# In-projection of the second block: operand sums, stores and loads regrouped among the engines

## The chip, the cores and the metric

The kernel runs on one core of a Trainium2 chip. The metric is the device time of one execution in microseconds (us), the median over several runs. The profile is that of one execution, read by engine: PE multiplies matrices (PEld loads its stationary operand), DVE is VectorE, ACT is ScalarE, POOL is GpSimd, SP is SyncE, which here only starts DMAs.

## What is computed

Two transformer blocks in sequence over 1,024 tokens of width 1,024, all in float32. Only the start of the second block matters here. With `x` the first block's output after its final norm:

```
hx = modulate(rmsnorm(x, norm1_g), sh1, sc1)
q, k, v, u, b, c, ga, gc = split(hx @ w_in)      # 1024, 256, 256, then 5 x 1024 columns
q, k = axial_rope(q), axial_rope(k)              # rotation
z = c * u;  y = b * conv3(z)                     # short convolution over tokens
a = (y @ w_proj_conv) * sigmoid(gc) + (attention(q, k, v) @ w_proj_attn) * sigmoid(ga)
x = x + g1 * (a @ w_out)                         # the residual is x itself
```

Attention over windows and a mixture of experts follow; they are not touched.

## The kernel before

**Float32 by three products.** Each operand is split into a high part, which ACT writes (line 58), and a remainder, which DVE writes (line 59); `mm3` (lines 65 to 67) adds three matmuls of 128x128 by 512. Weights arrive in the order of a list written by hand: `Weights.fill` has SP load the next 512 KB into one of four raw slots as soon as an earlier one has been split, `conv` splits the next piece, and `get` splits until `1 + ahead` pieces are ready and hands out one. The split pieces turn in a ring of three buffers, so a buffer comes free when PE has used the piece three before. Every engine works through its own instructions in the order of the program, and a DMA that SP or POOL starts waits its turn there.

**Order of the stage.** `x1` holds the first block's output, transposed, eight tiles of 128x1024.
1. `natural` for the 256 context rows: four pieces of K, a callback `mid` after some of them. After the second piece `x1_rs` makes row factors; after the third `hx_first` spreads one of them over a tile (`spread`: eight PE transposes into two PSUM banks, two ACT copies) and begins `hx`, the split modulated input, eight pairs of 128x1024 (lines 1238 to 1251).
2. A second row factor is spread to `rs1b` (line 1285), behind all of `hx` on ACT.
3. `natural` for keys and values (line 1317): 8 PSUM banks, one for each 128 tokens, four pieces of 48 matmuls, then `ev_kv` for each bank: DVE rotates the keys out of PSUM (lines 1292, 1296), POOL adds the two terms (line 1297) and starts the store, ACT copies the values.
4. `x1n` (line 1314): DVE scales the eight `x1` tiles by `rs1b`, and SP stores them as the residual. `x1`'s memory then goes to `TQ`, the operands of step 6.
5. `natural` twice for the queries, 512 columns each, with `ev_q` at the end of each (rotation as in 3, 512 wide; the tiles of the two terms and of the sum have two buffers each). In the first of the two, `quarters(k)` follows each of the four pieces: POOL adds high and low part of `hx` back together (line 1331, two of 128x1024) and forms four differences of quarters (line 1334, 128x512), which ACT and DVE split into `TQ`.
6. `quads` (line 1352): two blocks of 128 columns against all tokens with seven products instead of eight (Strassen's scheme in Winograd's form). Each product is 12 matmuls into a bank of its own; the banks turn through all eight. `SEVEN` says which quarters or sums each uses; the matching sums of the weights are made by `seven` on POOL: `make2` (lines 153, 154) for products 2 and 3, `make3` (158) for product 4, `make4` (162) for product 5. `W.ahead` goes to 4 ahead of the first `quads`.
7. Twenty calls of `quads`, the last four for the attention gate. In the last one `y_split` follows products 0 to 3: it splits a tile of `y` and calls `y_load`, in which POOL starts the load of the next one into the buffer that came free (one `y`, one `z`). The rest of the eight tiles follows after it. POOL's next DMAs load the keys and queries for the attention (`kn`, `qn`, lines 1502, 1503); SP's load the gate of the convolution (`gc_load`, line 1456), which `ev_mc` on DVE multiplies (line 1460). PE goes on with `y @ w_proj_conv`, first two column blocks with K as the outer loop (line 1516), then one block at a time.

Of the kernel before, what the change touches and what calls it, by code (L numbers as in the profile page):

```python
# [8 lines left out]
F32 = mybir.dt.float32  # L9
# [5 lines left out]
OP = mybir.AluOpType  # L15
# [3 lines left out]
P = 128  # L19
# [3 lines left out]
def fused(tc, x, mix_norm_g, w_in, b_f, sgu_ln_g, sgu_ln_b, w_s, b_s, out_norm_g, w_out,  # L23
# [4 lines left out]
    nc = tc.nc  # L28
# [3 lines left out]
    T, D = x.shape[1], x.shape[2]  # L32
    NT = T // P
    KD = D // P
    TH = T // 512
    EPS = 1e-6
    ACT, DVE, POOL, PE = nc.scalar, nc.vector, nc.gpsimd, nc.tensor
    act = nc.scalar.activation
    ES = ExitStack()
    L, R = "left", "right"  # L40

    def pool(es, name, bufs=1, side=L, space=None):
        kw = dict(name=name, bufs=bufs)
        if space is not None:
            kw["space"] = space
        else:
            kw["side"] = side
        return es.enter_context(tc.tile_pool(**kw))
# [4 lines left out]
    def rd(ap):  # L53
        return ap.bitcast(F32)

    def split(h, l, src, scale=None):
        if scale is None:
            act(h, src, AF.Copy)  # L58
            DVE.tensor_tensor(l, src, rd(h), op=OP.subtract)  # L59
        else:  # L60
            act(h, src, AF.Copy, scale=scale)
            DVE.scalar_tensor_tensor(l, src, scale, rd(h), op0=OP.mult, op1=OP.subtract)

    def mm3(ps, lh, ll, rh, rl, start, stop):
        PE.matmul(ps, lh, rh, start=start, stop=False)  # L65
        PE.matmul(ps, lh, rl, start=False, stop=False)  # L66
        PE.matmul(ps, ll, rh, start=False, stop=stop)  # L67
# [134 lines left out]
    def wsrc(w, k0, kc, c0, n):  # L202
        return w[k0 * P:(k0 + kc) * P, c0:c0 + n].rearrange("(k p) n -> p k n", p=P)
# [25 lines left out]
    def cols(n):  # L229
        a = small[:, nsm[0]:nsm[0] + n]  # L230
        nsm[0] += n
        assert nsm[0] <= 320
        return a
# [29 lines left out]
    def spread(dst, col, pts=None):  # L263

        for h in range(2):
            pt = pts[h] if pts else psb.tile([P, 512], F32, name="b")
            for t in range(4):
                PE.transpose(pt[:, t * P:(t + 1) * P], col[:, 4 * h + t:4 * h + t + 1].to_broadcast([P, P]), ident)
            act(dst[:, h * 512:(h + 1) * 512], pt, AF.Copy)
# [72 lines left out]
    W = Weights(es_a, units, stage=0, scols=1056)  # L342
# [12 lines left out]
    for src in (mix_norm_g, out_norm_g, ffn_norm_g, norm1_g_2, norm2_g_2, conv_w_2, b_mod_2, c_2, c_ctx_2):  # L355
        n = 1
# [102 lines left out]
    def natural(W, lH, lL, pieces, n, evac, nt=NT, mid=()):  # L459

        pss = [psb.tile([P, 512], F32, name="b") for _ in range(nt)]
        k0, K = 0, sum(pieces)
        for p, kc in enumerate(pieces):
            wh, wl = W.get()
            for t in range(nt):
                for kk in range(kc):
                    k = k0 + kk
                    mm3(pss[t][:, :n], lH(k, t), lL(k, t), wh[:, kk, :], wl[:, kk, :], k == 0, k == K - 1)
            k0 += kc
            if p in mid:  # L470
                mid[p]()
        for t in range(nt):
            evac(t, pss[t][:, :n])
# [49 lines left out]
    for g4 in range(2):  # L523
# [3 lines left out]
        o = slice(g4 * 4, g4 * 4 + 4)  # L527
# [382 lines left out]
    for i in range(NPART):  # L910
        n = -(-(FF - f0) // (NPART - i))
# [41 lines left out]
    es_x1 = ExitStack()  # L953
# [12 lines left out]
    for k in (6, 7):  # L966
        nc.sync.dma_start(raws[k], d_sgu[k - 4])
    groups = ((0, 3), (3, 3), (6, 2))
    W = Weights(es_m, [(wsrc(w_out, k0, kc, c0 * P, n * P), "k", 2) for c0, n in groups
                       for k0, kc in (((4, 4), (0, 4)) if c0 else ((6, 2), (0, 4)))],  # L970
                stage=2, scols=1536, pcols=768, name="w2")
# [50 lines left out]
    W = W3  # L1022
# [9 lines left out]
    es_f = ExitStack()  # L1032
    phh = pool(es_f, "phh", 5)
    for f in late:
        f(phh.tile([P, T], F32, name="hH")[:, :512])
    es_mo = ExitStack()
    rsb = s1

    def ffn_rs():
# [45 lines left out]
    def fw_done():  # L1085
        nonlocal psg, pmo
        es_fw.close()
        psg = pool(es_f, "psg", 2)
        pmo = pool(es_mo, "pmo", 2)

    psg = pmo = None
    for f0, n in parts:
        hT = []
        for f in range(f0, f0 + n):
# [20 lines left out]
            else:  # L1115
                columns_k(W, 2, xh, xhl, range(KD), lambda c, hf, ps: (ev_gate, ev_up)[c](hf, ps),
                          mid={(FM[0], 1): ffn_rs, (FM[1], 1): lambda: (spread(rsb, rs1), fw_done()), (FM[2], 1): lambda: W.prime(1)})
# [10 lines left out]
        mod_sum(modr.popleft())  # L1128
    assert not modq
    es_mo.close()  # L1130
    es_s1.close()


# [70 lines left out]
    d_y = dram.tile([KD, P, T], F32, name="d_y")  # L1204
# [6 lines left out]
    hx = []  # L1211
    ss3 = cols(16)
    rs3 = cols(16)
# [21 lines left out]
    def hx_mul(k, cs):  # L1235
        if k not in tmps:
            tmps[k] = tf("hH")
        DVE.scalar_tensor_tensor(tmps[k][:, cs], x1[k][:, cs], F1[:, k:k + 1], rsxb[:, cs], op0=OP.mult, op1=OP.mult)

    def hx_split(k, cs):  # L1240
        tmp, b1 = tmps[k][:, cs], B1[:, k:k + 1]
        if len(hx) == k:
            hx.append((xt(F32R), xt(F32R)))
        h, l = [a[:, cs] for a in hx[k]]
        if k in HP:
            act(tmp, tmp, AF.Identity, bias=b1)
            act(h, tmp, AF.Copy)
            POOL.tensor_tensor(l, tmp, rd(h), op=OP.subtract)
        else:
            act(h, tmp, AF.Identity, bias=b1)  # L1250
            DVE.scalar_tensor_tensor(l, tmp, b1, rd(h), op0=OP.add, op1=OP.subtract)

    whole = slice(0, T)
    HP = (3, 6)
    hs = [slice(0, 512), slice(512, 1024)]
    def hx_first():
        spread(rsxb, rs3[:, 8:])
        for c in hs:
            hx_mul(0, c)
        for c in hs:  # L1260
            hx_split(0, c)
        hx_mul(1, whole)

    natural(W, lambda k, t: hcH[:, k, t * P:(t + 1) * P], lambda k, t: hcL[:, k, t * P:(t + 1) * P], (2,) * 4, 512,
# [16 lines left out]
    rs_ = prp.tile([P, NT, 64], F32, name="rs", bufs=1)  # L1281
    nc.gpsimd.dma_start(rc, ropec_h)
    nc.gpsimd.dma_start(rs_, ropes_h)
    rs1b = pool(es_x1, "prs1", 1, R).tile([P, T], F32, name="rs1b")
    spread(rs1b, rs3[:, :8])

    def rope(dst, t, ps, nh):
        n = nh * 64
# [10 lines left out]
    hl_ = lambda k, t: hx[k][0][:, t * P:(t + 1) * P]  # L1299
    hll = lambda k, t: hx[k][1][:, t * P:(t + 1) * P]  # L1300
# [7 lines left out]
    def ev_q(c, t, ps):  # L1308
        qo = prp.tile([P, 512], F32, name="qo")
        rope(qo, t, ps, 8)  # L1310
        nc.gpsimd.dma_start(d_q[:, t, c:c + 512], qo)

    def x1n(k):
        DVE.scalar_tensor_tensor(x1[k], x1[k], fngT[:, k:k + 1], rs1b, op0=OP.mult, op1=OP.mult)  # L1314
        nc.sync.dma_start(d_x1T[k], x1[k])

    natural(W, hl_, hll, (2,) * 4, 512, ev_kv)
    for k in range(KD):
        x1n(k)
    es_x1.close()  # L1320


# [2 lines left out]
    TQ = [[pT.tile([P, 4, 512], F32R, name=f"T{i}{c}") for c in "hl"] for i in range(1, 5)]  # L1325

    def quarters(k):
        tr = prp.tile([P, 4, 512], F32, name="tr", bufs=1)
        for i in range(2):
            h, l = hx[k + 4 * i]  # L1330
            POOL.tensor_tensor(tr[:, 2 * i:2 * i + 2, :].rearrange("p i n -> p (i n)"), rd(h), rd(l), op=OP.add)  # L1331
        a11, a12, a21, a22 = [tr[:, i, :] for i in range(4)]
        for o, x, y in ((a11, a12, a11), (a12, a22, a12), (a22, a22, a11), (a21, a21, a22)):
            POOL.tensor_tensor(o, x, y, op=OP.subtract)
        for (h, l), t in zip(TQ, (a11, a22, a12, a21)):
            split(h[:, k, :], l[:, k, :], t)

    for c in (0, 512):
        natural(W, hl_, hll, (2,) * 4, 512, lambda t, ps: ev_q(c, t, ps),
                mid={} if c else {i: (lambda i=i: quarters(i)) for i in range(4)})  # L1340
    es_rp.close()


# [27 lines left out]
    def plus(o, s, b):  # L1371
        DVE.tensor_tensor(o, s, b, op=OP.add)
        return o
# [3 lines left out]
    for j in range(8):  # L1377
# [9 lines left out]
        y = pcv.tile([P, T], F32, name="y")  # L1387
# [14 lines left out]
    def y_load():  # L1402
        k = len(ys) + len(yraw)
        t = pcv.tile([P, T], F32, name="y") if k % 2 else pcv.tile([P, T + 2], F32, name="z")[:, :T]
        nc.gpsimd.dma_start(t, d_y[k])
        yraw.append(t)

    def y_split():
        ys.append((xt(F32R), xt(F32R)))
        split(*ys[-1], yraw.popleft())  # L1410
        if len(ys) + len(yraw) < KD:
            y_load()

    for j in range(4):
        ga, gb = [pcv.tile([P, T], F32, name="g", bufs=2) for _ in range(2)]
        g1, g2 = half("c1"), half("c2")
        mid = {}
        if j == 3:

            W.ahead = 2  # L1420
            mid = {i: (lambda: y_split()) for i in range(4)}
        quads(lambda s, b: act(ga[:, h0], plus(g1, s, b), AF.Sigmoid), lambda s, b: act(ga[:, h1], plus(s, s, b), AF.Sigmoid),
              lambda s, b: act(gb[:, h0], plus(s, s, b), AF.Sigmoid), lambda s, b: act(gb[:, h1], plus(g2, s, b), AF.Sigmoid), mid)
        for i, g in enumerate((ga, gb)):
            nc.gpsimd.dma_start(d_ga[2 * j + i], g)
        if j == 1:
            y_load()
            y_load()
# [519 lines left out]
    for r in range(P // 8):  # L1948
        o = slice(8 * r, 8 * r + 8)
# [123 lines left out]
    for t in range(NT + 2):  # L2073
        if t < NT:
            for c in hs:
                ps = psb.tile([P, 512], F32, name="b")
# [75 lines left out]
```

## Time and profile before

| | before |
|---|---|
| median of 3 runs (lowest to highest) | 3036.11 us (3034.88 to 3037.55) |
| the profiled execution: its time / span | 3037.48 / 3035.7 us |
| mean granted clock of PE | 0.976 of full speed |
| busy: PE / DVE / ACT / POOL | 2868.3 (94%) / 1900.1 (63%) / 1361.9 (45%) / 649.0 (21%) us |
| HBM read / written | 380.62 / 58.23 MB |

The span runs from the first to the last instruction; the time is 1.78 us longer. Starts below are us from the span's start. The work of steps 1 to 7 above begins at about 1230 us, the last `quads` ends at about 1812 us. In a list of waits each line gives who waited, for whom, the total us, the number of times and the longest one. In a timeline: start, duration, engine, line, what it writes and reads, and in brackets how long the engine had been idle and what released it.

### The profile page before, as it was taken

What the parts mean: (1) busy time and instruction counts of PE and PEld (TensorE: products, weight loads), DVE (VectorE), ACT (ScalarE), POOL (GpSimd) and SP (SyncE); (2) the same over time, 40 slices, a digit from 0 to 9 for tenths busy, and PEclk for the clock granted to TensorE, in tenths of its full rate; (3) what the DMA queues carried; (4) which work ended last, traced back from release to release, by engine and by line L of the source; (5) the groups of instructions that cost most, each with busy time, mean ns of one, the idle gap of its engine ahead of it and who ended that gap; (6) DMA issues with size and microseconds to landing.
All of it is one profiled execution on the core that took longest, in us unless ns stands there. A gap on an engine that the chain in (4) does not pass through costs nothing.

```text
span 3035.7 us, 37203 instructions
## 1 busy us (share of the span) xinstructions
PE 2868.3 (94%) x13943; PEld 2392.6 (79%) x13943; DVE 1900.1 (63%) x2717; ACT 1361.9 (45%) x2127; POOL 649.0 (21%) x639
## 2 busy tenths in 40 slices
PE   9999999999999999868999998899899879999997
PEld 7987878888888888756888877777778668888885
DVE  4446944645344445554666652789742479999998
ACT  5346933111121113320322231688721368888886
POOL 2201312000000001275444421133221301211113
PEclk9999999999999999988999999999999889999999
DMA  5120141222232222232222246000253589999998
GB/s 198 36 77 22 41 148 49 90 84 94 72 100 75 92 83 63 76 118 84 83 84 84 83 156 230 25 15 22 71 181 137 194 313 368 377 371 378 377 377 288
DMA packets 295236, 441.27 MB, mean 145 GB/s; under 512 B 14300, under 2 KB 143040, under 8 KB 294928
## 3 DMA queue, kind: packets, MB, share of 16 engines
q1 hardware_dynamic: 276896, 375.54, 35.8%
q0 software_dynamic: 16672, 62.31, 6.0%
q8 instruction: 109, 1.79, 0.2%
q10 hardware_dynamic: 1488, 1.06, 0.1%
q14 instruction: 71, 0.58, 0.1%
HBM read 380.62 MB, written 58.23 MB: 145 GB/s over the span
## 4 chain that ended last, share of the span: by engine, by line
PE 80%; DVE 8%; ACT 4%; POOL 3%; DMA 3%; issue 3%; SPq 0%; POOLq 0%; ACTq 0%; DVEq 0%
PE b L65 23%; PE b L67 23%; PE b L66 23%; PE pt L1612 2%; PE b L1993 1%; PE po L1642 1%; DVE wl L59 1%; PE po L1643 1%; PE pt L777 1%; POOL qo L1297 1%; DVE x L1314 1%; POOL tr L1331 1%; DVE qs L1497 1%; DVE pl L1630 0%; PE sp L1582 0%
## 5 line engine op out<-in xcount | busy, mean ns | idle before, releaser
L59 DVE TENSOR_TENSOR wl<-wst,wh 128x1024 fp32r<-128x1024 f32 (+3 forms) x620 | 713.7, 1180 | 283.1 <-ACT wh L58 275.1
L58 ACT ACTIVATE wh<-wst 128x1024 fp32r<-128x1024 f32 (+3 forms) x620 | 595.1, 976 | 472.2 <-PE b L66 194.9
L67 PE MATMUL b<-xn,wl 128*128 128x512 f32 x1040 | 407.0, 391 | 10.5 <-DVE wl L59 10.5
L65 PE MATMUL b<-xn,wh 128*128 128x512 f32 x1040 | 407.6, 392 | 2.4 <-ACT wh L58 2.4
L66 PE MATMUL b<-xn,wh 128*128 128x512 f32 x1040 | 405.9, 390 | 0.0
L65 PE MATMUL b<-wh,a 128*128 128x512 f32 x768 | 302.2, 394 | 0.2 <-ACT a L58 0.2
L66 PE MATMUL b<-wl,a 128*128 128x512 f32 x768 | 299.7, 390 | 0.8 <-DVE wl L59 0.8
L67 PE MATMUL b<-wh,a 128*128 128x512 f32 x768 | 299.6, 390 | 0.4 <-DVE a L59 0.4
L67 PEld LDWEIGHTS b<-xn,wl 128*128 128x128 f32 x1040 | 196.1, 189 | 53.6 <-DVE wl L59 12.4
L65 PEld LDWEIGHTS b<-xn,wh 128*128 128x128 f32 x1040 | 196.3, 189 | 43.5 <-ACT wh L58 3.3
L66 PEld LDWEIGHTS b<-xn,wh 128*128 128x128 f32 x1040 | 196.1, 189 | 40.4
L241 POOL TENSOR_SCALAR small<-small 128x1 f32<-128x1 f32 (+3 forms) x15 | 5.7, 382 | 766.9 <-ACT xn L1155 680.1
L67 PEld LDWEIGHTS b<-wh,a 128*128 128x128 f32 x768 | 144.4, 188 | 31.0 <-DVE a L59 1.1
L66 PEld LDWEIGHTS b<-wl,a 128*128 128x128 f32 x768 | 144.6, 188 | 30.6 <-DVE wl L59 1.6
L65 PEld LDWEIGHTS b<-wh,a 128*128 128x128 f32 x768 | 144.6, 188 | 29.6 <-ACT a L58 0.7
L2035 POOL DMA_INDIRECT d_x<-b,idxT x15 | 65.8, 4388 | 470.4 <-DVE b L2029 470.4
L65 PE MATMUL b<-hH,wh 128*128 128x512 f32 x352 | 137.7, 391 | 0.0
L67 PE MATMUL b<-hH,wl 128*128 128x512 f32 x352 | 137.1, 389 | 0.0
L66 PE MATMUL b<-hL,wh 128*128 128x512 f32 x352 | 137.0, 389 | 0.0
L58 ACT ACTIVATE hH<-sg 128x512 fp32r<-128x512 f32 x44 | 27.8, 632 | 202.7 <-DVE sg L1108 202.7
L1101 ACT ACTIVATE sg<-sg 128x512 f32<-128x512 f32 x44 | 27.7, 632 | 179.7 <-DVE sg L1100 179.7
L65 PE MATMUL b<-wh,xn 128*128 128x512 f32 x192 | 77.3, 403 | 32.6 <-DVE t L1296 24.2
(569 smaller groups left out, 6383.3 us busy)
## 6 DMA issues: line engine op xcount, KB each, us to landing
wst<-in_w_exp_gate_dram SPq DMA_DIRECT2D x128, 512.0 KB, 10.8
wst<-in_w_exp_up_dram SPq DMA_DIRECT2D x128, 512.0 KB, 10.8
wst<-in_w_exp_down_dram SPq DMA_DIRECT2D x128, 512.0 KB, 10.8
wst<-in_w_in_dram SPq DMA_DIRECT2D x74, 512.0 KB, 4.0
mw<-in_w_mod_dram SPq DMA_DIRECT2D x48, 512.0 KB, 5.0
wst<-in_w_gate_up_dram SPq DMA_DIRECT2D x44, 512.0 KB, 4.0
wst<-in_w_down_dram SPq DMA_DIRECT2D x16, 512.0 KB, 3.8
wst<-in_w_out_dram SPq DMA_DIRECT2D x10, 512.0 KB, 4.1
```

Of the source, the lines that this page charges most:

```text
L58: act(h, src, AF.Copy)
L59: DVE.tensor_tensor(l, src, rd(h), op=OP.subtract)
L65: PE.matmul(ps, lh, rh, start=start, stop=False)
L66: PE.matmul(ps, lh, rl, start=False, stop=False)
L67: PE.matmul(ps, ll, rh, start=False, stop=stop)
L777: PE.transpose(pt[:, b * P:(b + 1) * P], sm[:, (k0 + b) * P:(k0 + b + 1) * P], ident)
L1297: POOL.tensor_tensor(dst, t1, t2, op=OP.add)
L1314: DVE.scalar_tensor_tensor(x1[k], x1[k], fngT[:, k:k + 1], rs1b, op0=OP.mult, op1=OP.mult)
L1331: POOL.tensor_tensor(tr[:, 2 * i:2 * i + 2, :].rearrange("p i n -> p (i n)"), rd(h), rd(l), op=OP.add)
L1497: DVE.tensor_tensor(q[64:128, cs], pt[64 * o:64 * o + 64], rd(q[0:64, cs]), op=OP.subtract)
L1612: PE.transpose(pt[:, hh * P:(hh + 1) * P], sms[4 * u + hh][:, kb * P:(kb + 1) * P], ident)
L2035: nc.gpsimd.indirect_dma_start(out=d_x2, out_offset=bass.IndirectOffsetOnAxis(ap=idxT[:, e:e + 1], axis=0), in_=y, in_offset=None, compute ...
```

## The change

- `rs1b` is spread inside `hx_first`, after the first tile of `hx` and ahead of the other seven. To make room for it, the pool `psg` of the feed-forward is closed earlier.
- `x1n` is called in `mid` of the keys' and values' pass, two tiles after each piece, not after the pass.
- `quarters` runs its six additions and subtractions on DVE, not on POOL, and splits its results in the order in which they are made. It is called after the first three pieces of the first query pass and after the first piece of the second.
- `W.ahead` becomes 4 after the third piece of the second query pass, ahead of its last piece and of its rotation.
- `y_load` is started by SP, not by POOL, and the four `y_split` of the last `quads` follow products 0, 1, 3 and 4.

```diff
@@ feed-forward
-    es_mo = ExitStack()
+    es_sg, es_mo = ExitStack(), ExitStack()
-        psg = pool(es_f, "psg", 2)
+        psg = pool(es_sg, "psg", 2)
     es_mo.close()
+    es_sg.close()
@@ hx_first
+    rs1b = pool(es_x1, "prs1", 1, R).tile([P, T], F32, name="rs1b")
         for c in hs:
             hx_split(0, c)
+        spread(rs1b, rs3[:, :8])
         hx_mul(1, whole)
...
-    rs1b = pool(es_x1, "prs1", 1, R).tile([P, T], F32, name="rs1b")
-    spread(rs1b, rs3[:, :8])
@@ keys and values
-    natural(W, hl_, hll, (2,) * 4, 512, ev_kv)
-    for k in range(KD):
-        x1n(k)
+    natural(W, hl_, hll, (2,) * 4, 512, ev_kv, mid={i: (lambda i=i: (x1n(2 * i), x1n(2 * i + 1))) for i in range(4)})
@@ quarters
-            h, l = hx[k + 4 * i]
-            POOL.tensor_tensor(tr[:, 2 * i:2 * i + 2, :].rearrange("p i n -> p (i n)"), rd(h), rd(l), op=OP.add)
+            DVE.tensor_tensor(tr[:, 2 * i:2 * i + 2, :].rearrange("p i n -> p (i n)"), *[rd(a) for a in hx[k + 4 * i]], op=OP.add)
-            POOL.tensor_tensor(o, x, y, op=OP.subtract)
-        for (h, l), t in zip(TQ, (a11, a22, a12, a21)):
+            DVE.tensor_tensor(o, x, y, op=OP.subtract)
+        for i, t in ((0, a11), (2, a12), (1, a22), (3, a21)):
+            h, l = TQ[i]
             split(h[:, k, :], l[:, k, :], t)
-    for c in (0, 512):
-        natural(W, hl_, hll, (2,) * 4, 512, lambda t, ps: ev_q(c, t, ps),
-                mid={} if c else {i: (lambda i=i: quarters(i)) for i in range(4)})
+    mids = {i: (lambda i=i: quarters(i)) for i in range(3)}
+    natural(W, hl_, hll, (2,) * 4, 512, lambda t, ps: ev_q(0, t, ps), mid=mids)
+
+    mids = {0: lambda: quarters(3), 2: lambda: setattr(W, "ahead", 4)}
+    natural(W, hl_, hll, (2,) * 4, 512, lambda t, ps: ev_q(512, t, ps), mid=mids)
@@ the gates' end
-        nc.gpsimd.dma_start(t, d_y[k])
+        nc.sync.dma_start(t, d_y[k])
-            mid = {i: (lambda: y_split()) for i in range(4)}
+            mid = {i: y_split for i in (0, 1, 3, 4)}
```

## Rows read from the trace of the kernel before

**Rows 1.** The page, part 4: the chain that ended last, by engine.
```profile
PE 80%; DVE 8%; ACT 4%; POOL 3%; DMA 3%; issue 3%; SPq 0%; POOLq 0%; ACTq 0%; DVEq 0%
```

**Rows 2.** PE's waits from 1240 to 1440 us.
```profile
PE b L65 <- DVE t L1296: 24.2, 3, 22.7
PE b L65 <- ACT wh L58: 7.6, 1, 7.6
PE b L65 <- ACT rs1b L269: 7.0, 1, 7.0
...
PE b L66 <- DVE wl L59: 1.0, 1, 1.0
```

**Rows 3.** Busy times 1430 to 1790 us: PE, PEld, DVE, ACT, POOL, PEclk, DMA share, GB/s.
```profile
1430.00:1790.00 360.00, 360.00 (x1582) 297.88 (x1581) 230.60 (x305) 110.90 (x187) 158.60 (x122) 1.00 0.28 89
```

**Rows 4.** Timeline of PE: start of step 3, and the matmuls after three waits.
```profile
1243.49 0.48 PE L65 MATMUL b<-wh,xn 128*128 128x512 f32 x1
...
1261.54 0.80 PE L65 MATMUL b<-wh,xn 128*128 128x512 f32 x1 [6.98 <-ACT rs1b L269]
...
1366.90 0.77 PE L65 MATMUL b<-wh,xn 128*128 128x512 f32 x1 [22.69 <-DVE t L1296]
...
1428.30 0.79 PE L65 MATMUL b<-T2h,wh 128*128 128x512 f32 x1 [7.62 <-ACT wh L58]
...
1433.67 0.39 PE L65 MATMUL b<-T1h,wh 128*128 128x512 f32 x1
```

**Rows 5.** Timeline of DVE, the last tile of `hx`.
```profile
1260.09 2.18 DVE L1251 SCALAR_TENSOR_TENSOR xn<-hH,modT,xn 128x1024 fp32r<-128x1024 f32 x1 [1.22 <-ACT xn L1250]
```

**Rows 6.** Lines 1314 and 59, DVE: count, ns shortest/median/longest, first and last start.
```profile
L1314 DVE SCALAR_TENSOR_TENSOR x<-x,small,rs1b x8: 1276/2308/3415, 1302.1 to 1317.8; 128x1024 f32<-128x1024 f32 x8
L59 DVE TENSOR_TENSOR wl<-wst,wh x4: 1210/1219/2304, 1320.0 to 1352.5; 128x1024 fp32r<-128x1024 f32 x4
L59 DVE TENSOR_TENSOR T3l<-tr,T3h x4: 677/678/685, 1324.9 to 1364.2; 128x512 fp32r<-128x512 f32 x4
```

**Rows 7.** Lines 1331 and 1297, POOL, in the same form.
```profile
L1331 POOL TENSOR_TENSOR tr<-xn x8: 2334/2854/3411, 1306.5 to 1355.8; 128x1024 f32<-128x1024 f32 x8
L1297 POOL TENSOR_TENSOR qo<-t,t x16: 1252/1294/1372, 1366.8 to 1422.8; 128x512 f32<-128x512 f32 x16
```

**Rows 8.** The chain from 1200 to 1500 us: start, us, what.
```profile
1365.49 0.60 DVE t L1292
...
1405.83 0.69 DVE t L1292
...
1424.97 1.27 POOL ws L153
```

**Rows 9.** Timelines of PE and DVE, last `quads` and the columns after it.
```profile
1799.41 0.50 PE L65 MATMUL b<-T3h,wh 128*128 128x512 f32 x1 [1.06 <-ACT wh L58]
...
1804.68 0.50 PE L65 MATMUL b<-xn,wh 128*128 128x512 f32 x1 [1.97 <-ACT wh L58]
...
1840.62 1.28 DVE L1460 TENSOR_TENSOR g<-g,b 128x512 f32<-128x512 f32 x2 [12.16 <-DMA g<-d_gc]
...
1845.59 0.80 PE L67 MATMUL b<-xn,wl 128*128 128x512 f32 x1 [9.49 <-DVE wl L59]
```

**Rows 10.** Timeline of POOL in the last `quads`.
```profile
1796.86 0.54 POOL L1405 DMA_DIRECT2D y<-d_y  x1 [2.93 <-DVE xn L59]
1797.41 1.29 POOL L158 TENSOR_TENSOR wst<-wst 128x512 f32<-128x512 f32 x1
...
1821.69 0.54 POOL L1503 DMA_DIRECT2D qn<-d_q  x1
```

**Rows 11.** DMA issues from 1700 to 1870 us: count, KB each, median us to landing.
```profile
qn<-d_q POOLq DMA_DIRECT2D x1, 4096.0 KB, 18.1
g<-d_gc SPq DMA_DIRECT2D x5, 512.0 KB, 14.1
...
y<-d_y POOLq DMA_DIRECT2D x4, 512.0 KB, 5.0
```

## The prediction, made before the change was run

> **What bounds the kernel now.** The chain that ended last runs 80% of its length through PE [rows 1], so PE's idle time is what there is to gain, and after it the time that PE runs slowly. I read PE's waits for the stretch of the change first [rows 2], then PE's timeline at each of them [rows 4], then DVE, ACT and POOL just ahead. PE undisturbed is seen in the sevens: 1582 matmuls in 360 us at clock 1.00 [rows 3], 0.2275 us each, though the other engines do the same kinds of work there. Against that the projection loses in three large places.
>
> - Keys and values: 7.0 us until ACT has written `rs1b` [rows 2, 4]. The pass needs all eight banks, and the two that `spread` took come free behind all of `hx` on ACT.
> - Between the two query passes: 22.7 us for a rotation term [rows 2, 4]. The banks are full and DVE begins the rotation only at 1365.5 [rows 8], because the fourth set of sums stands ahead of it, and that set waits on POOL (two additions of 2.3 to 3.4 us and four subtractions, [rows 7]).
> - At product 2 of the sevens: 7.6 us for ACT [rows 2, 4]; its weight sum is made on POOL at 1424.97, behind the whole rotation [rows 8].
>
> After such a wait PE runs slowly. Twelve matmuls from 1428.30 to 1433.67 [rows 4] take 5.37 us where twelve at full speed take 2.73: 2.65 us more. I charge that for each of the three waits.
>
> **The change, part by part.** All sums are against the profiled execution (3037.5 us; span 3035.7 and 1.8 around it), which is 1.4 above the median. I take the gain from the median.
>
> *Row factor early.* Eight PE transposes and two ACT copies are moved, none added. The copies now stand ahead of ACT's part of the second `hx` tile, which PE awaits already, so I charge 0.2 us. The two banks are free long before the pass reaches them. Does another wait take over? PE starts the pass at 1243.5 [rows 4] and uses two `hx` tiles per piece of 48 x 0.2275 = 10.9 us, so the last two are wanted 32.8 us later, at 1276. They are done at 1262.3 [rows 5]. Gain 7.0 + 2.65 - 0.2 = **9.4**. Bounds: 0 (if `hx` is late after all) and 9.6.
>
> *Residual with the keys.* Eight DVE instructions move from 1302-1320, where they took 1.28 to 3.4 us beside POOL's additions [rows 6], to gaps of the keys' pass. There POOL has little, so I take 1.28: 10.2 us among some 47 of PE's time. The last two stand ahead of the keys' rotation and delay it by 2.6 us; PE needs the banks one per 1.36 us (six matmuls) after the pass ends, and the rotation of a bank begins 9.5 us before that, so the delay is covered. SP's eight stores move ahead of weight loads; a load is wanted two pieces (22 us) after it, which covers a wait for one DVE instruction. What goes: PE's 1.0 us wait for a weight remainder, which stood behind these instructions on DVE. Gain **1.0**; bounds -2 and 1.0.
>
> *Sums on DVE.* A set is two additions of 128x1024, priced like DVE's remainder of a weight, 1.22 us [rows 6]; four subtractions and four remainders of 128x512 at 0.68, or 0.6 back to back. That is 2.4 + 4.9 = 7.3 us, and 8.5 with the remainder of the piece that lies between two sets. A piece lasts 10.9 us on PE, so DVE keeps up. By the clock of the new run: keys' pass over at about 1289.6 (1243.5, 192 x 0.2275, 2.3 us of small waits that stay), first set begins at about 1299.7 behind the keys' rotation and one weight, three sets and two weights later it is 1324.0, with the last weight 1325.2. The first query bank is ready at 1323.7, so the rotation starts 1.5 us late. It then goes at POOL's pace, 1.29 for the addition [rows 7] and 0.9 to start the store, 2.2 us per bank, two buffers ahead, and DVE leaves the eighth bank at about 1340.1. PE wants that bank 9.5 us into the next pass, at 1342.6: 2.5 us to spare, so with sets of p us PE waits 3(p - 7.3) - 2.5 = 3p - 24.4. So the 22.7 us go, and so do the other two waits of that row, 24.2 - 22.7 = 1.5. The fourth set lies in the second pass, where DVE has little else. Gain 24.2 + 2.65 = **26.8**. Bounds: sets of 13 us (all at line 1314's median to its shortest, 2.31 / 1.28 = 1.8 times) make PE wait 14.6 with a slow start, which leaves 9.6; no wait gives 26.8.
>
> *Weight sums ahead.* `make2` now runs on POOL while it is idle, and product 2 has its weights in time. The split buffer for them comes free with the third piece of the pass, hence no earlier than its last. Next comes product 4: its `make3` is the first thing on POOL after the rotation. From the first rotation on DVE to a free POOL it took 1405.83 to 1424.97, 19.1 us [rows 8]; the first bank is ready 1.4 us into the last piece, two remainders of 0.7 go first on DVE, then `make3` 1.3 and ACT 0.6: 1.4 + 0.8 + 19.1 + 1.9 = 23.2 us after that piece's start. PE gets to product 4 after 10.9 + 4 x 2.73 = 21.8. With the remainder on DVE behind it I take a new wait of 2.0. Gain 7.6 + 2.65 - 2.0 = **8.3**; bounds 0 and 10.3.
>
> *The loads of y by SP.* In the last `quads` POOL's `make3` runs at 1797.41 behind two loads that waited for DVE [rows 10], and `make4` likewise; PE waits 1.06 and 1.97 for what follows [rows 9]. With SP waiting in POOL's place both go. After the second PE slowed too, for which I take half of 2.65. Gain **4.4**, bounds 2 and 5.7. On SP, weight loads are queued behind such a load, but four raw slots are ahead of PE.
>
> *After the gates.* PE waits 9.49 us for a remainder [rows 9] that is queued on DVE behind the multiplication by the gate, and that waits for a load of 14.1 us [rows 9, 11] running beside the 4 MB of the queries (18.1 us, issued at 1821.69) [rows 10, 11]. Without the last `y` loads ahead of it POOL starts the queries' load some 4 us sooner beyond PE's own shift, so the gate lands sooner; but the last two `y` loads now run beside it. I take half, **4**; bounds -5 and 12.
>
> Skill and trace: these loads took 5.0 us ahead of the queries' and SP's gate load 14.1 beside it [rows 11]. The Trainium skill, DMA: Bandwidth & Descriptors (Issuing engines are not separate DMA queues), says that all issuing engines end on the same 16 DMA engines and that several save only the issuing time. By it this last gain would be nothing or a loss; the row decides for a part, since the order of issue changes too.
>
> Sum: 9.4 + 1.0 + 26.8 + 8.3 + 4.4 + 4 = 53.9, so 3036.1 - 53.9 = **2982**. Everything behind waits for this stage's results, and I see nothing there that starts on its own.
>
> **Rivals.**
> 1. *The y loads collide.* They take 14.1 instead of 5.0 beside the queries' load, 9.1 us; the gate's load, which needs their buffers, moves by that. The last gain turns from 4 to -5: 2991. For it: the gate's row [rows 11]. Against: they are issued close to the start of that load, where the last one of before landed after about 6.
> 2. *DVE stays late in the first query pass* (sets of 9 to 12 us): PE waits 3p - 24.4 at the pass boundary, 3 to 12, in the middle 7, and with a slow start 10: 2992. For it: the contended durations [rows 6]. Against: POOL has no additions while the first three sets run.
> 3. *The sums are not ahead.* If the split buffer comes free later than I read, ACT and DVE stand before it with the rotation behind them, and product 2 waits as before: 2982 + 8.3 = 2990.
> 4. *Slower: DVE becomes the bound.* The same formula from far larger sets. The three sets cost 3p - 24.4 at the boundary. The fourth delays the last weight of the second pass: 9.5 + 1.2 + p + 1.2 against 32.7 us, so p - 20.8. Two slow starts cost 5.3: 4p - 39.9 in all. That passes the 53.9 from p = 23.5. At 28 it costs 72.1 and gives 3054. Against: even if every instruction took line 1314's longest to its shortest, 2.7 times, p would be 20. By the Trainium skill, SBUF — State Buffer (SBUF: two separate sides), a DVE instruction with two SBUF inputs is shut out by GpSimd for a whole instruction; the trace agrees in 1.28 against 2.3 and 3.4 us. That takes a POOL instruction each time, and the change removes them from this stretch.
> 5. *Nothing arrives at the end*, if some later stream of weights sets the end whatever PE does: 3036.
>
> **How the numbers follow.** Chances: forecast 0.62, rivals 0.17, 0.09, 0.07, 0.03, 0.02. The forecast's own bounds: best case, no wait at product 4 (2.0), the full 5.7 at the loads and the full 12 after the gates give 63 to 65, so 2971; two unfavourable terms together (no gain from the row factor, a collision of 9) leave 35, so 3001. Range 2970 to 3002, which takes in rivals 1 to 3. A measurement tells 0.2%, about 6 us, from no change: faster 0.95, same 0.02, slower 0.03.
>
> **What would show it.** Right: no wait for `rs1b`, none over 3 us between the query passes, clock 1.00 from there into the sevens; a new wait of about 2 us at product 4; line 1331 on DVE near 1.2 us and no line under the x1 tiles over 1.4; POOL without gaps before `make3` in the last `quads`. Wrong: a wait for a rotation term at the pass boundary (rival 2), product 2 still waiting (3), or landings of `y` above 10 us with PE waiting in the first two columns (1).

## The result, and the profile after

The changed kernel takes **2989.43 us** (median of 4 runs, 2987.73 to 2993.21), the kernel before 3036.83 in the same comparison: 47.4 us less, ratio 0.9846 with a 95% interval of 0.9829 to 0.9863. The forecast was 2982, the range 2970 to 3002. The profiled execution took 2987.78 us with a span of 2985.8.

What PE waits for from the context's pass into the sevens, after (the view of [rows 2]: who, for whom, total us, times, longest):

```profile
PE b L67 <- DVE wl L59: 1.6, 1, 1.6
PE b L65 <- ACT wh L58: 1.6, 1, 1.6
PE b L65 <- ACT xn L1251: 1.4, 1, 1.4
PE b L67 <- DVE xn L1252: 0.7, 1, 0.7
```

The 24.2, 7.6, 7.0 and 1.0 us of [rows 2] are gone. The last two lines were there before, with the same 1.4 and 0.7 us (L1250 and L1251 there). The first two are new, both at product 4 of the sevens. At the gates' end two waits have taken the place of the one of 9.49 us in [rows 9]:

```profile
PE b L65 <- ACT xn L58: 5.8, 1, 5.8
PE b L67 <- DVE wl L59: 3.2, 2, 2.7
```

To say where the 47.4 us came from, I cut both traces at three matmuls that both have: the last one ahead of PE's first wait in the keys' pass, the sixth of the first columns after the gates, ahead of a wait there, and the one ahead of its first wait in the attention (starts in the timeline of PE).

| stretch | before | after | difference | forecast |
|---|---|---|---|---|
| keys' pass to the first columns | 1244.03 to 1813.28: 569.25 | 1243.52 to 1763.65: 520.13 | -49.1 | -49.9 |
| first columns to the attention | 1813.28 to 1913.97: 100.69 | 1763.65 to 1867.54: 103.89 | +3.2 | -4 |

The spans differ by 49.9 us (3035.7, 2985.8): 0.5 ahead of the first cut, 45.9 in the two stretches, and 3.5 behind the attention's begin, which was not traced. Five of the six terms came as a whole within 0.8 us, and the sixth has the other sign. The five can be told apart as well, by matmuls counted from the first cut (us, starts in the timeline of PE):

| part of the first stretch, term | before | after | difference | forecast |
|---|---|---|---|---|
| to the 100th: row factor | 1244.03 to 1278.77: 34.74 | 1243.52 to 1270.48: 26.96 | -7.8 | -9.4 |
| to the 300th: residual | to 1325.46: 46.69 | to 1315.82: 45.34 | -1.4 | -1.0 |
| to the 480th: sums on DVE | to 1393.77: 68.31 | to 1356.62: 40.80 | -27.5 | -26.8 |
| to the 700th: weight sums ahead | to 1454.11: 60.34 | to 1410.24: 53.62 | -6.7 | -8.3 |
| to the sixth of the columns: loads of `y` | to 1813.28: 359.17 | to 1763.65: 353.41 | -5.8 | -4.4 |

So the 0.8 is partly luck: single terms are off by up to 1.6 us, both ways. The first one lacks 1.6 us because PE's clock fell there in this execution (last section). In an execution where it did not, that of keys and queries by SP below, the part takes 25.38 us (1242.15 to 1267.53), 9.4 less than before, as forecast. Now the other terms one by one. Timeline of DVE after, the second and third set of sums and the begin of the rotation (start, duration, what; the last bracket is idle time before it and its releaser):

```profile
1309.23 2.35 DVE L1330 TENSOR_TENSOR tr<-xn 128x1024 f32<-128x1024 f32 x2
1311.50 2.86 DVE L1333 TENSOR_TENSOR tr<-tr 128x512 f32<-128x512 f32 x4
...
1316.69 1.22 DVE L59 TENSOR_TENSOR wl<-wst,wh 128x1024 fp32r<-128x1024 f32 x1
1317.82 2.35 DVE L1330 TENSOR_TENSOR tr<-xn 128x1024 f32<-128x1024 f32 x2
...
1326.41 0.68 DVE L1294 TENSOR_TENSOR t<-b,rc 128x512 f32<-128x512 f32 x1
...
1340.67 0.74 DVE L1298 TENSOR_TENSOR t<-b,rs 128x256 f32<-128x256 f32 x2
```

A set and its weight repeat every 8.6 us (1309.23 to 1317.82), where 8.5 was forecast. The rotation begins at 1326.41 (forecast 1325.2, before 1365.5 [rows 8]) and leaves the last bank at 1341.4 (forecast 1340.1). PE does not wait there at all, and its granted clock is 1.00 from 1260 to 1740 us. The residual's eight instructions now take 1.27 us each, 1279 ns the longest, where the longest of [rows 6] was 3415:

```profile
L1316 DVE SCALAR_TENSOR_TENSOR x<-x,small,rs1b x8: 1272/1274/1279, 1262.9 to 1283.6; 128x1024 f32<-128x1024 f32 x8
```

Product 4, from the timelines of POOL, ACT, DVE and PE after, each in its own fence.

```profile
1386.36 1.30 POOL L1299 TENSOR_TENSOR qo<-t,t 128x512 f32<-128x512 f32 x1
...
1388.54 1.28 POOL L158 TENSOR_TENSOR wst<-wst 128x512 f32<-128x512 f32 x1
```
```profile
1389.85 0.63 ACT L58 ACTIVATE wh<-wst 128x512 fp32r<-128x512 f32 x1 [21.37 <-POOL wst L158]
```
```profile
1390.67 3.85 DVE L59 TENSOR_TENSOR wl<-wst,wh 128x512 fp32r<-128x512 f32 x2
```
```profile
1390.53 0.50 PE L65 MATMUL b<-T3h,wh 128*128 128x512 f32 x1 [1.57 <-ACT wh L58]
1392.88 0.50 PE L67 MATMUL b<-T3h,wl 128*128 128x512 f32 x1 [1.62 <-DVE wl L59]
```

POOL's `make3` (line 158) follows the last rotation term directly, ACT splits it, PE starts: the wait of about 2 us that was forecast. It became 3.2 because DVE's remainder took 1.9 us (3.85 for two) in place of 0.68 [rows 6]: POOL was making the next sums beside it. The Trainium skill, SBUF — State Buffer (SBUF: two separate sides), has DVE, when both its inputs lie in SBUF, shut out for a whole instruction by a GpSimd instruction that reads SBUF and started first; 1.9 us agrees, as 0.68 and one of POOL's sums of 1.28 make 1.96.

The second stretch is read best from ACT, SP and POOL and from the DMA issues (count, KB each, median us to landing) around 1764 to 1792 us after:

```profile
1785.76 1.06 ACT L58 ACTIVATE xn<-z 128x1024 fp32r<-128x1024 f32 x1 [16.42 <-DMA z<-d_y]
1789.65 1.06 ACT L58 ACTIVATE xn<-y 128x1024 fp32r<-128x1024 f32 x1 [2.84 <-DMA y<-d_y]
```
```profile
1769.67 0.34 SPq L1407 DMA_DIRECT2D z<-d_y  x1
1770.81 0.34 SPq L1407 DMA_DIRECT2D y<-d_y  x1
```
```profile
qn<-d_q POOLq DMA_DIRECT2D x1, 4096.0 KB, 20.2
...
kn<-d_kv POOLq DMA_DIRECT2D x1, 1024.0 KB, 10.7
```
```profile
1768.26 0.93 POOL L1504 DMA_DIRECT2D kn<-d_kv  x1
1769.18 0.55 POOL L1505 DMA_DIRECT2D qn<-d_q  x1
```

SP started the last two `y` loads at 1769.67 and 1770.81, and ACT could use them at 1785.76 and 1789.65: 16 and 19 us, where such a load took 5.0 [rows 11]. POOL had started the keys' and queries' loads at 1768.26 and 1769.18, before them. PE reached the seventh `y` tile at 1781 and waited.

### The profile page after: what moved, and what is told of

Same layout as the page of the kernel before. It is cut to its first block, busy times and chain, and to the rows that moved or that the text cites. A ratio compares the mean times of both kernels' runs of the same rounds, so it can differ in the third digit from the quotient of the medians.

```text
span 2985.8 us, 37222 instructions
## 1 busy us (share of the span) xinstructions
PE 2859.5 (96%) x13943; PEld 2389.1 (80%) x13943; DVE 1911.1 (64%) x2741; ACT 1362.7 (46%) x2127; POOL 596.9 (20%) x607
## 3 DMA queue, kind: packets, MB, share of 16 engines
q10 hardware_dynamic: 1488, 1.06, 0.1%
## 4 chain that ended last, share of the span: by engine, by line
PE 81%; DVE 7%; ACT 4%; issue 4%; DMA 3%; POOL 1%; SPq 0%; POOLq 0%; DVEq 0%; ACTq 0%
PE b L67 24%; PE b L65 24%; PE b L66 24%; PE pt L1614 1%; DVE pl L1632 1%; PE b L1995 1%; DVE sm L1595 1%; PE po L1644 1%; DVE wl L59 1%; DVE qs L1499 1%; PE pt L777 1%; DMA y<-d_y 1%; DMA d_x<-b,idxT 1%; PE po L1645 1%; PE b L1837 0%
## 5 line engine op out<-in xcount | busy, mean ns | idle before, releaser
L1595 DVE CUSTOM_DVE_ANT_0 sm<-sp,mk,nsk 128x640 f32<-128x640 f32 (+1 forms) x128 | 107.0, 837 | 1.2 <-PE sp L1584 1.0
```

The source lines that it names most:

```text
L1595: DVE.tensor_tensor_reduce(sms[n][:, :nk], sps.pop(n)[:, 256:256 + nk], (mk if i else mk0)[:, :nk], -0.125, nsk[:, hd:hd + 1], op0=OP.add, ...
```

## Experiments

All of them change the kernel after, except one that changes the kernel before. The cut table above serves for them too: "first stretch" is the time from the keys' pass to the first columns (520.1 after), "second" that from there to the attention (103.9).

### Who pays at the gates' end

**The loads of y by POOL again.**
```diff
-        nc.sync.dma_start(t, d_y[k])
+        nc.gpsimd.dma_start(t, d_y[k])
```


> The changed kernel with the loads of y started by POOL again, everything else changed. Theory (the last two y loads lose because the loads of keys and queries are already running when they start): with POOL as issuer they stand ahead of the keys' and queries' loads again, land in 4 to 6.5 us, and PE's wait of 5.8 us for the split of y goes; the queries' load then runs beside the gate's, so the wait of 2.7 us for a weight remainder grows to about 9; make3 waits for a y load on POOL again, about 1 us of PE at product 4 of the last seven. Net within 3 us of the changed kernel (2989). Rival (SP's queue as such is what made the y loads slow, and POOL is simply better): the same landing, but a net gain of 6 to 9 us.

Measured 2989.23 us (2988.81 to 2992.0), the same as after. The issues from 1740 to 1800 us, and PE's waits from 1700 to 1850:

```profile
qn<-d_q POOLq DMA_DIRECT2D x1, 4096.0 KB, 18.2
...
z<-d_y POOLq DMA_DIRECT2D x3, 512.0 KB, 4.4
y<-d_y POOLq DMA_DIRECT2D x3, 512.0 KB, 3.7
```
```profile
PE b L67 <- DVE wl L59: 11.0, 4, 9.7
PE b L65 <- ACT wh L58: 2.1, 2, 1.1
```

POOL starting the last `y` load and the queries' load, and ACT when that `y` has landed:

```profile
1772.15 0.53 POOL L1407 DMA_DIRECT2D y<-d_y  x1 [0.60 <-DVE xn L59]
...
1773.59 0.54 POOL L1505 DMA_DIRECT2D qn<-d_q  x1
```
```profile
1778.08 1.06 ACT L58 ACTIVATE xn<-y 128x1024 fp32r<-128x1024 f32 x1 [0.37 <-DMA y<-d_y]
```

As expected: `y` lands quickly again (5.9 us from issue to use for the last one), the wait for its split is gone, and the wait behind the gate's load is 9.7 us, as before the change. The first stretch is 522.5 us (1242.15 to 1764.63), 2.4 more than after, the second 102.1 (to 1866.70), 1.8 less: together 624.6 for 624.0. Between these two orders of issue the loss only moves from one transfer to another.

The run also parts the term of the `y` loads in two. From product 2 of the last `quads` to the sixth of the columns PE takes 20.5 us before (1792.75 to 1813.28), 17.5 here (1747.18 to 1764.63) and 14.8 after (1748.88 to 1763.65). So 3.1 of the 5.8 us come without SP, from the new places of `y_split`: the wait of 1.97 us does not return, the one of 1.06 does. The issuer brings the other 2.7.

**Keys and queries by SP, behind the gate.**
```diff
-    nc.gpsimd.dma_start(kn, d_kv[:, :, :256])
-    nc.gpsimd.dma_start(qn, d_q)
+    nc.sync.dma_start(kn, d_kv[:, :, :256])
+    nc.sync.dma_start(qn, d_q)
...
```
(likewise the three loads of the mask)

> The changed kernel with the loads of keys, queries and mask started by SP, in SP's order behind the last y loads and the first two gate loads. Theory (collision): the last two y loads land in 3 to 4.5 us, the gate in 3 to 6, and the waits of 5.8, 0.5 and 2.7 us and the slow start after them (2.65) go: 9 to 12 us faster than the changed kernel, about 2979. Rival (loads of y started by SP are slow whatever runs beside them): y lands in 16 us again and the time stays at 2989.

Measured 2977.37 us (2971.15 to 2985.66), ratio to before 0.9814 (0.9799 to 0.9829): 12 us faster than after. SP and ACT there:

```profile
1768.12 0.34 SPq L1407 DMA_DIRECT2D z<-d_y  x1
1769.26 0.34 SPq L1407 DMA_DIRECT2D y<-d_y  x1
1776.76 0.79 SPq L1458 DMA_DIRECT2D g<-d_gc  x2
1777.65 0.61 SPq L1504 DMA_DIRECT2D kn<-d_kv  x1
```
```profile
1773.19 1.06 ACT L58 ACTIVATE xn<-z 128x1024 fp32r<-128x1024 f32 x1 [5.40 <-DMA z<-d_y]
1774.41 1.06 ACT L58 ACTIVATE xn<-y 128x1024 fp32r<-128x1024 f32 x1 [0.16 <-DMA y<-d_y]
```

The same loads by the same SP are used 5.1 us after their issue (1768.12 to 1773.19), so SP's queue is not what was slow. PE waits 2.0 us for weight remainders (the 2.7 us of after have become 1.5, and had been expected to go) and for no split of `y`; the second stretch takes 91.2 us (1762.07 to 1853.30), 12.7 less than after. The collision is shown. Which of the five loads that were moved does it was not parted; the queries' is 4,096 of their 5,696 KB. Nor was a `y` load of POOL's behind the queries' tried.

### The steps of the first stretch, one taken back at a time

**Sums on POOL, at their new places.**
```diff
-            DVE.tensor_tensor(tr[...], ..., op=OP.add)
+            POOL.tensor_tensor(tr[...], ..., op=OP.add)
-            DVE.tensor_tensor(o, x, y, op=OP.subtract)
+            POOL.tensor_tensor(o, x, y, op=OP.subtract)
```


> The changed kernel with the six additions and subtractions of a set on POOL again, at their new places. Theory (the engine counts, as DVE does a set in 7.3 us and POOL took 13.1 with the splits): three sets end some 14 us later, DVE's rotation of the first query pass starts that much later, and PE waits 11 to 14 us at the pass boundary with a slow start: 12 to 17 us slower than the changed kernel, about 3004. Rival (the new places do it: three sets ahead of the rotation in place of four, and no residual on DVE in between): within 3 us of the changed kernel.

Measured 3002.21 us (2995.22 to 3002.32), 12.8 over after; the first stretch is 533.5 us (1243.40 to 1776.91), 13.4 more. PE's waits from 1232 to 1440 us:

```profile
PE b L65 <- DVE t L1298: 9.3, 4, 8.0
```

The engine counts: with POOL a wait at the boundary is back, though only three sets stand ahead of the rotation. It is less than the 11 to 14 us expected, and less than the 24 us of before, where a fourth set and the residual stood ahead as well; what each of these two makes of the difference was not tried with POOL.

**The engine alone, in the kernel before.** The same two lines of `quarters` on DVE and nothing else of the change.

> The kernel before with the six additions and subtractions of a set on DVE and nothing else changed: four sets still ahead of the rotation, the residual still on DVE behind the keys' pass. Theory (DVE is the path there, whatever engine makes the sums): the residual ends about 1312, four sets of 7.3 and their weights end about 1348, PE waits 8 to 11 us in all at the pass boundary in place of 24: 14 to 18 us faster than before, about 3021. Rival (the engine alone gives the whole 26.8 us): 3010. The waits of 7.0 for the row factor and 7.6 at product 2 stay in both.

Measured 3019.25 us (3017.43 to 3020.49), ratio 0.994 (0.9924 to 0.9957), 16.6 us under before. PE's waits there:

```profile
PE b L65 <- ACT wh L58: 7.7, 1, 7.7
PE b L65 <- DVE t L1296: 7.5, 3, 6.6
PE b L65 <- ACT rs1b L269: 7.0, 1, 7.0
```

So the engine alone gives 16.6 us, of 26.8 forecast for the whole term; a wait of 7.5 us stays, with its slow start, and needs the other moves. The fourth set was not moved by itself, so how these share it is not shown. The two other waits stand untouched, as they should.

**The residual behind the keys' pass.**
```diff
-    natural(W, hl_, hll, (2,) * 4, 512, ev_kv, mid={...})
+    natural(W, hl_, hll, (2,) * 4, 512, ev_kv)
+    for k in range(KD):
+        x1n(k)
```


> The changed kernel with the scaling and store of the residual behind the keys' pass again. Theory (the gap of DVE between the passes has 2.5 us to spare): eight instructions of 1.28 us, less the 2.5 that no longer stand ahead of the keys' rotation, and the wait for the last store before the sums may be written make the sets 6 to 9 us later; PE waits 3 to 6 us at the pass boundary: 3 to 9 us slower than the changed kernel. Rival (the sets have more room than that): same as the changed kernel.

Measured 2993.59 us (2991.26 to 2999.51), 4.2 over after, though the executions of the two overlap. PE waits at the boundary four times, 2.3 us together, less than the 3 to 6 expected:

```profile
PE b L65 <- DVE t L1298: 2.3, 4, 0.6
```

The first stretch is 523.5 us (1244.98 to 1768.44), 3.3 more. Counted from that first cut, DVE's rotation begins 5.8 us later than after (88.73 us behind it for 82.89). Short waits cost PE more than their idle time: from the 300th to the 480th matmul it takes 44.5 us (1317.25 to 1361.76) for 40.8, so it is 3.7 us late. The spare time at the boundary is what is left, some 2.1 us.

**Longer sets.** The size of that spare decides how near the change is to losing, so it was measured once more, with each set's two additions carried out three times.
```diff
+            for _ in range(3):
-            DVE.tensor_tensor(tr[...], ..., op=OP.add)
+                DVE.tensor_tensor(tr[...], ..., op=OP.add)
```


> The changed kernel with the two additions of each set carried out three times (the same result), so that a set takes 7.3 + 2 x 2.35 = 12.0 us on DVE. The prediction's formula 3p - 24.4 gives a wait of 11.6 us at the boundary of the query passes, which with a slow start makes 12 to 15 us over the changed kernel, about 3003. Rival (the rotation has more room, as PE wants the banks later than the formula has it): a wait under 6 us and a time under 2996.

Measured 2999.61 us (2998.43 to 3002.42), 10.2 over after, less than the 12 to 15 expected. The rotation begins 96.44 us behind the first cut (1342.00 - 1245.56). Unlike after, this execution lost no time to PE's clock ahead of the 100th matmul (25.35 us, 1245.56 to 1270.91), so its match is the run of keys and queries by SP, where the rotation begins 81.43 us behind the cut (1323.58 - 1242.15), 15.0 earlier. DVE in this run, then in that one, and PE's wait:

```profile
1342.00 0.68 DVE L1294 TENSOR_TENSOR t<-b,rc 128x512 f32<-128x512 f32 x1
```
```profile
1323.58 0.68 DVE L1294 TENSOR_TENSOR t<-b,rc 128x512 f32<-128x512 f32 x1
```
```profile
PE b L65 <- DVE t L1298: 10.3, 4, 8.5
```

From the 300th to the 480th matmul PE takes 53.8 us (1316.24 to 1370.06), 13.0 more than after, and 15.0 - 13.0 gives 2.0 us of spare, as the run above. With the sums on POOL it is 2.3 in the same way: the rotation 14.6 us later than after (1340.92 - 1243.40), PE 12.3 (1315.69 to 1368.81). The formula came within 1.2 us: 3p - 24.4 with a slow start gave 11.6 + 2.65 = 14.2 us, and the part became 13.0 longer. The first stretch is 531.4 us, only 11.3 more, as after lost 1.6 us to its clock ahead of it.

**The row factor late.**
```diff
         for c in hs:
             hx_split(0, c)
-        spread(rs1b, rs3[:, :8])
         hx_mul(1, whole)
...
     nc.gpsimd.dma_start(rs_, ropes_h)
+    spread(rs1b, rs3[:, :8])
```


> The changed kernel with the row factor spread behind all of the input's splits again. Theory: PE's wait of 7.0 us for the two banks and its slow start of about 2.4 return and nothing else changes: 9 us slower than the changed kernel, about 2998. Rival (the gain of this step depends on the others, since there is time to spare before the query passes): 0 to 4 us slower.

Measured 2995.5 us (2991.33 to 2998.83), 6.1 over after. The wait is back in full (`ACT rs1b`, 7.0 us), and the first stretch is 527.7 us (1244.77 to 1772.48), 7.6 more. After lost 1.6 us to its clock in the part concerned; against the run of keys and queries by SP, which did not, the part up to the 100th matmul is 34.85 us (1244.77 to 1279.62) for 25.38, 9.5 more, where 9 was expected.

**The lead late.**
```diff
-    mids = {0: lambda: quarters(3), 2: lambda: setattr(W, "ahead", 4)}
+    mids = {0: lambda: quarters(3)}
```


> The changed kernel without the early rise of the weights' lead, so that the first sums are made behind the rotation of the second query pass. Theory: product 2 waits about 7.6 us with a slow start of 2.65, and the 3.2 us at product 4 go: 6 to 8 us slower than the changed kernel, about 2996. Rival (the sums' split is held back by the buffer ring anyway, and the lead brings little): within 3 us.

Measured 2994.57 us (2991.78 to 2997.33), 5.1 over after. PE waits 7.4 us at product 2 and not at all at product 4, as expected. The first stretch is 525.2 us (1244.90 to 1770.06), 5.0 more; the part from the 480th to the 700th matmul is 60.3 (1356.37 to 1416.67), 6.7 more, within the 6 to 8 expected.

### A version beyond both

**Sums of product 4 and 5 first.** POOL makes them ahead of the rotation, and the first is split ahead of the sevens' own tiles.
```diff
+    def sums_first():
+        for i in range(2):
+            f, n = W.todo[i]
+            W.todo[i] = (lambda v=f(): v, n)
+
-    mids = {0: lambda: quarters(3), 2: lambda: setattr(W, "ahead", 4)}
+    mids = {0: lambda: quarters(3), 2: lambda: setattr(W, "ahead", 4), 3: sums_first}
     natural(W, hl_, hll, (2,) * 4, 512, lambda t, ps: ev_q(512, t, ps), mid=mids)
+    W.prime(5)
     es_rp.close()
```


> The changed kernel with POOL's make3 and make4 of the first seven placed ahead of the rotation of the second query pass, and the split of make3's result ahead of the first instruction of the seven's own tiles. Theory (product 4 waits because make3 is POOL's first work after the rotation): the waits of 1.6 and 1.6 us at product 4 go, nothing takes their place: 3 to 4 us faster than the changed kernel, 2986. Rival (the wait is for memory that the rotation's last store still holds): at least 2 of the 3.2 us stay, 2988.

Measured 2984.68 us (2978.62 to 2985.66), 4.7 under after. PE has no wait at product 4; its first stretch takes 514.9 us (1242.18 to 1757.04), 5.3 less than after; 1.6 of these are the clock's, told at the end.

**Both edits.** This, and keys and queries by SP.

> The changed kernel with both edits: make3 and make4 ahead of the rotation, and the loads of keys, queries and mask started by SP behind the gate's first loads. If the two waits are independent, the gains add: 12 to 15 us faster than the changed kernel, about 2976, and PE has no wait over 1.5 us from the keys' pass to the attention. If the time lost at the gates' end comes back later (the attention waits for queries that land later), only 3 to 6 us.

Measured **2969.8 us** (2966.98 to 2972.98), ratio to before 0.978 (0.9767 to 0.9793), an interval that lies wholly under that of the change. PE's waits from 1232 to 1440 us are these and no others, and then those from 1700 to 1850:

```profile
PE b L65 <- ACT xn L1251: 1.4, 1, 1.4
PE b L67 <- DVE xn L1252: 0.7, 1, 0.7
```
```profile
PE b L67 <- DVE wl L59: 2.0, 2, 1.5
PE b L65 <- ACT wh L58: 1.0, 1, 1.0
```

The gains add: 12.1 and 4.7 alone, 19.6 together, which is 3 more than their sum and more than expected. The profiled executions differ by 15.4 us (2972.36, 2987.78), and up to the attention the two stretches are 516.4 and 91.2 us, 16.4 under after. So those two executions show no gain beyond these stretches, and the 3 us lie within the spread of the runs (3 to 15 us within one kernel here).

## Why the prediction was right, and where it was not

- **Row factor early: right.** No wait took its place; taking it back brings 7.0 us of wait and 9.5 in its part at the same clock, of 9.4 forecast.
- **Residual with the keys: right.** 1.27 us each, against 1.28 forecast, no wait behind them, and 1.4 us gained for 1.0. Behind the pass they would now cost PE 3.7 us at the boundary.
- **Sums on DVE: right**, in price (8.6 for 8.5 us with a weight), in time (1326.4 for 1325.2) and in effect. The experiments add that the engine alone gives 16.6 us. Rival 2 and the slower rival 4 hang on the spare time at the boundary: 2.0 to 2.3 us in three runs, forecast as 2.5, so both lie about where I had them.
- **Weight sums ahead: right in mechanism**, including the new wait at product 4. That wait was mis-sized, 3.2 us for 2.0, and the term came as 6.7 for 8.3: I let the remainder on DVE cost its undisturbed 0.68, though POOL goes on with the next sums at that moment.
- **The loads of y by SP: right in time, 5.8 for 4.4, and half right in cause.** PE's waits of 1.06 and 1.97 us are gone, but only the first returns when POOL starts the loads: the other needed no SP, only the new places of `y_split`, to which the prediction gave no term.
- **After the gates: wrong in sign.** The step that failed is "I take half, 4": I weighed the earlier queries' load against the last two `y` loads beside it and let the first win. The stretch lost 3.2 us. What I held against the collision, that the last `y` load of before landed after about 6 us close to the start of that load, did not carry over: POOL had started that one 1.4 us ahead of the queries' (1820.25 and 1821.69), and after the change SP starts it 1.6 us behind. Rival 1 (0.17) describes it, with its -5; its price of 14.1 us for a load was too small, 16 to 19 were measured. What saved its size is that the gate's load, which now starts when the queries' are through, landed in 4.6 us in place of 14.1. By the sentence from the Trainium skill, DMA: Bandwidth & Descriptors (Issuing engines are not separate DMA queues), the change of issuer would bring nothing or a loss there; the stretch agrees, 103.9 us with SP and 102.1 with POOL.

In all: 49.1 - 3.2 = 45.9 us up to the attention, 53.9 forecast, 47.4 in the median.

## What to carry to other kernels

When a buffer is freed late, follow it back to the engine whose queue the freeing instruction stands in, and count how long that queue is in the new order: here the price of each queue, added up by hand, gave the start of the rotation to 1.2 us. A transfer that is moved to another queue leaves its place in the order of issue as well; look at what now starts ahead of it, above all at a transfer of megabytes that nobody needs soon, and put that one last. Work that an idle engine could do early is worth placing ahead of that engine's next long series, even if only two instructions are moved.

## What was not expected of the hardware

A load of 512 KB started 0.5 to 1.6 us behind one of 4 MB (and one of 1 MB ahead of that) took 16 and 19 us, nearly as long as the large one (20.2); the forecast had counted on 5 to 14.

The clock fell after waits that had not made it fall before. PE's two waits of 1.4 and 0.7 us at the start of the keys' pass are in all runs. Windows of 10 us (busy of PE, PEld, DVE, ACT, POOL, then clock, DMA share, GB/s), after, and then keys and queries by SP:

```profile
1240.00:1250.00 10.00, 7.93 (x32) 5.86 (x30) 9.65 (x10) 8.09 (x13) 0.00 (x0) 0.89 0.01 2
1250.00:1260.00 10.00, 10.00 (x43) 8.18 (x42) 8.75 (x7) 6.23 (x7) 5.10 (x2) 0.94 0.00 0
```
```profile
1240.00:1250.00 10.00, 7.88 (x34) 5.89 (x33) 9.75 (x9) 8.29 (x12) 1.04 (x1) 1.00 0.01 2
1250.00:1260.00 10.00, 10.00 (x46) 8.29 (x45) 8.75 (x6) 6.40 (x7) 4.79 (x2) 1.00 0.00 0
```

With the same code up to there, one execution keeps the full 2.4 GHz and the other drops to 1.2 for part of the time (matmuls 0.43 us apart for 0.23) and loses some 1.6 us. At product 4 it is the other way round: behind waits of 1.36 and 1.61 us the run of keys and queries by SP has a granted clock of 0.83 from 1390 to 1400 us, and after, behind 1.57 and 1.62, has 1.00. So a slow start behind a short wait is no fixed price, and terms of 2 us that rest on it cannot be told apart here in one execution.
